# Strassen-type FFN products on one core: sums and forms on VectorE, raw weights in 512-column pieces, four pairs begun early

## The chip, the cores and the metric

The kernel runs on one NeuronCore of a Trainium2 chip. The metric is the device time of one execution in microseconds (us), smaller being better. The core has TensorE (PE, matrix products; PEld is its weight load), VectorE (DVE), ScalarE (ACT), GpSimd (POOL) and SyncE (SP, which here issues nearly all DMAs). Each engine works through its own instructions in order, and waits where an operand is not there yet.

## The reference

One layer of an encoder, for 512 prompt tokens and 256 sample tokens with the same weights, model width 1024, FFN width 2816, all in float32:

```python
x = layer_norm(ALPHA * x + 0.5 * swiglu(x, ffn1_up, ffn1_down), ln1_g, ln1_b)
u = x @ w_in
...
h_a = rwkv7_branch(u_a, ...) @ w_branch_a
h_b = retention_branch(u_b, pos) @ w_branch_b
mix = (sigmoid(gate_a) * h_a + sigmoid(gate_b) * h_b) @ w_out
x = layer_norm(ALPHA * x + mix, ln2_g, ln2_b)
x = layer_norm(ALPHA * x + 0.5 * swiglu(x, ffn2_up, ffn2_down), ln3_g, ln3_b)
```

with swiglu(x) = (silu(x W_gate) * (x W_up)) W_down. The prompt and the sample attend only within themselves.

## The kernel before

All tiles hold features on the 128 partitions and the T = 768 tokens (512 + 256, SEGS) along the columns; x is eight tiles z[0..7]. A float32 matrix product is made of three products of rounded parts: every operand is split into a high part (a cast on ACT, L187) and a low part (source minus high part on VectorE, L188), and PE multiplies high by high, high by low and low by high (mm3, mmt, L198). High and low parts are named xh/xl (tokens), ph/pl (weights), eh/el (forms of the tokens), hh/hl (hidden units) and wh/wl (weights of other stages).

The stages, by the trace's time: FFN1 (`first`, 0 to 525 us); LN1 with two leading input projections (to 581); the RWKV and retention preparation and the scan (to about 1240); `merge` with w_out and LN2 (to about 1432); FFN2 (to 1944); LN3 and the stores (to 1984). A scheduler orders each engine's instructions from the program's text and its own costs, so the order is not that of the text.

**FFN up products.** The gate and up weights of a block of hidden units and the tokens are cut into halves and multiplied by a Winograd form of Strassen's scheme: seven products in place of eight. For each of the 22 pairs j, `head(j)` makes product 11 and copies it to u; `second(j)` adds product 21 in the same PSUM bank and applies silu; `do_up(j)` makes four sums of raw weights (`combine`, tiles sa, on POOL, L329), then products T1, T3, T2, 22 and T4, five adds of 384 columns on VectorE (L360), a product of 768 columns (L371) and the split into hh and hl. Each product is 12 matmuls of 384 columns. `forms` (L276 to L291) makes for each of the four k four forms of the tokens, two on POOL (L282, L283) and two on VectorE (L284, L285), and splits them.

**FFN down products.** Chunks of 6, 6, 5 and 5 pairs: after the first pair of the next chunk, `do_down` adds the chunk's share of all eight z. The last chunk's down product is made per token segment (`last_down`), with LN's token sums behind it. Weights split for the first segment are held for the second (KEEP = 4 in a pool of their own, and two more in the rotating pool).

**Buffers.** Raw up weights have three buffers wr of 1024 columns (512 KB, one DMA each); the four sums have buffers sa; ph and pl four each. The pools fw (raw, sums, split weights) and xe (forms) are closed before the last down, whose weights come through another pool, wp. Before the loop over chunks, two pairs have head and second done in FFN1, four in FFN2 (LEAD2). In PSUM, mm tiles are two banks wide (down products), pc one bank (up products and token sums); FFN1 and the preparation, and `merge` and FFN2, have different shares of the eight banks.

**LN.** Mean and variance are sums over all features, so over the partitions of eight tiles: either eight adds on VectorE into acc (L246) and one product with a matrix of ones on PE (L248), or eight such products on PE (L239). MPE and VPE say which, by LN and token segment. Then 1/sqrt on ACT and VectorE (L230 to L234), the scaling (L267 on VectorE, L268 on ACT) and, for LN1, stores of x to DRAM (x1d) and the split of x.

## Time and profile before

| | us |
|---|---|
| median of 3 runs (lowest, highest) | 1990.48 (1988.84, 1992.99) |
| the profiled execution | 1985.87 |
| its span, first to last instruction | 1984.1 |
| PE busy in the span | 1870.1 (94%) |
| DVE busy | 1240.4 (63%) |
| ACT busy | 833.2 (42%) |
| POOL busy | 486.5 (25%) |

The mean granted TensorE clock is 0.971 of full speed. A busy share is an average over stages with different limits, so the table alone does not say what a change is worth: that is read from the windows (busy time and counts in stretches of the span), from the chain of waits (the work that ended last, followed back) and from single rows of the timeline. In a row, the part in square brackets is the idle time of that engine just before and what ended it.

### The profile page before, as it was taken

The numbers are of one execution on the slowest core, as the hardware profiler recorded it, in microseconds if no ns is written. First come the engines' busy times: TensorE is split into PE (matmuls) and PEld (weight loads), VectorE is DVE, ScalarE is ACT, GpSimd is POOL, SyncE is SP. The second block draws the span as 40 slices with busy tenths as digits, with TensorE's granted clock in tenths as the row PEclk, the third lists the DMA queues.
The fourth block names the chain that finished last, engine by engine and source line by source line (L and its number), as shares of the span: only waits on it lengthen the run. The fifth ranks groups of instructions, "written<-read, shape, count | busy, mean of one in ns | idle before, by whom it ended". The sixth has DMA issues, their size and how long they took to land.

```text
span 1984.1 us, 33432 instructions
## 1 busy us (share of the span) xinstructions
PE 1870.1 (94%) x13224; PEld 1681.4 (85%) x13224; DVE 1240.4 (63%) x2064; ACT 833.2 (42%) x1512; POOL 486.5 (25%) x482
## 2 busy tenths in 40 slices
PE   6999999999979999999999988999779999999996
PEld 6999999999758777887888777789679999899985
DVE  8753745646675786768445556487777456365567
ACT  4432423424364453445355645334644234243334
POOL 5412303222000264445510000000164033131310
PEclk8999999999989999999999989999889999999998
DMA  4221221221242433333464442554222212212122
GB/s 133 75 67 62 76 74 64 61 78 46 79 143 86 148 117 127 109 129 116 142 207 127 128 114 90 196 194 146 75 76 72 78 64 71 69 64 74 65 68 73
DMA packets 115100, 197.48 MB, mean 100 GB/s; under 512 B 52736, under 2 KB 61312, under 8 KB 114944
## 3 DMA queue, kind: packets, MB, share of 16 engines
q1 hardware_dynamic: 97408, 173.32, 27.5%
q0 software_dynamic: 3424, 14.94, 2.3%
q10 hardware_dynamic: 14112, 7.08, 1.3%
q8 instruction: 105, 1.72, 0.4%
q14 instruction: 51, 0.42, 0.1%
HBM read 153.62 MB, written 41.68 MB: 98 GB/s over the span
## 4 chain that ended last, share of the span: by engine, by line
PE 81%; DVE 8%; ACT 4%; DMA 3%; issue 2%; POOL 1%; ACTq 0%; SPq 0%; DVEq 0%; POOLq 0%
PE mm L198 39%; PE pc L198 30%; PE pc L102 2%; PE mm L464 2%; ACT z L268 1%; PE pc L891 1%; POOL sa L329 1%; PE w L827 1%; PE w L838 1%; PE pc L939 1%; DMA wr<-in_f2u 1%; DVE z L259 1%; PE w L832 1%; PE pc L521 1%; DMA t<-gd 1%
## 5 line engine op out<-in xcount | busy, mean ns | idle before, releaser
L198 PE MATMUL pc<-xh,ph 128*128 128x384 f32 x704 | 241.4, 343 | 30.4 <-ACT xh L187 12.9
L187 ACT CAST ph<-wr 128x512 fp32r<-128x512 f32 (+1 forms) x228 | 129.1, 568 | 300.5 <-PE mm L198 180.2
L188 DVE TENSOR_TENSOR pl<-wr,ph 128x512 fp32r<-128x512 f32 (+1 forms) x228 | 174.7, 768 | 125.3 <-ACT ph L187 109.6
L198 PE MATMUL pc<-xl,ph 128*128 128x384 f32 x704 | 240.1, 341 | 0.2 <-DVE xl L188 0.2
L329 POOL TENSOR_TENSOR sa<-wr 128x512 f32<-128x512 f32 x44 | 70.1, 1593 | 626.5 <-DMA wr<-in_f1u 290.2
L360 DVE TENSOR_TENSOR u<-u,pc 128x384 f32<-128x384 f32 x220 | 121.0, 550 | 161.5 <-PE pc L198 160.0
L198 PE MATMUL mm<-xh,wh 128*128 128x512 f32 (+1 forms) x672 | 188.2, 356 | 18.1 <-ACT xh L187 8.5
L187 ACT CAST ph<-sa 128x512 fp32r<-128x512 f32 x176 | 109.2, 621 | 222.5 <-PE pc L198 160.0
L198 PE MATMUL mm<-xl,wh 128*128 128x512 f32 (+1 forms) x672 | 180.5, 346 | 2.6 <-DVE xl L188 2.6
L198 PE MATMUL pc<-eh,ph 128*128 128x384 f32 x528 | 178.0, 338 | 4.4 <-DVE u L360 4.1
L198 PE MATMUL pc<-el,ph 128*128 128x384 f32 x528 | 177.5, 336 | 0.2 <-DVE el L188 0.2
L188 DVE TENSOR_TENSOR pl<-sa,ph 128x512 fp32r<-128x512 f32 x176 | 143.3, 816 | 48.6 <-ACT ph L187 28.0
L198 PEld LDWEIGHTS pc<-xh,ph 128*128 128x128 f32 x704 | 135.9, 193 | 33.7 <-ACT xh L187 13.6
L158 ACT CAST wh<-wr 128x1024 fp32r<-128x1024 f32 (+2 forms) x96 | 85.7, 892 | 179.7 <-PE mm L198 133.0
L159 DVE TENSOR_TENSOR wl<-wr,wh 128x1024 fp32r<-128x1024 f32 (+2 forms) x96 | 100.9, 1051 | 93.4 <-PE mm L198 41.3
L198 PE MATMUL pc<-xh,pl 128*128 128x384 f32 x704 | 152.3, 338 | 3.1 <-DVE pl L188 3.1
L198 PEld LDWEIGHTS mm<-xh,wh 128*128 128x128 f32 x672 | 107.4, 192 | 42.6 <-ACT xh L187 9.7
L198 PE MATMUL mm<-hh,ph 128*128 128x512 f32 (+1 forms) x544 | 138.9, 336 | 0.0
L198 PE MATMUL mm<-hl,ph 128*128 128x512 f32 (+1 forms) x544 | 138.8, 336 | 0.0
L198 PEld LDWEIGHTS pc<-xl,ph 128*128 128x128 f32 x704 | 135.9, 193 | 0.6 <-DVE xl L188 0.6
L198 PE MATMUL mm<-xh,wl 128*128 128x512 f32 (+1 forms) x672 | 134.1, 348 | 0.0
L198 PEld LDWEIGHTS pc<-xh,pl 128*128 128x128 f32 x704 | 126.2, 190 | 3.7 <-DVE pl L188 3.7
(290 smaller groups left out, 4108.3 us busy)
## 6 DMA issues: line engine op xcount, KB each, us to landing
wr<-in_f2u SPq DMA_DIRECT2D x48, 512.0 KB, 3.5
wr<-in_f1u SPq DMA_DIRECT2D x44, 512.0 KB, 3.4
wr<-in_w_in SPq DMA_DIRECT2D x32, 512.0 KB, 3.5
wr<-in_w_out SPq DMA_DIRECT2D x16, 512.0 KB, 3.6
wr<-in_w_in SPq DMA_DIRECT2D x28, 256.0 KB, 3.4
wr<-in_f1d SPq DMA_DIRECT2D x16, 384.0 KB, 3.2
dd<-ar SPq DMA_DIRECT2D x8, 768.0 KB, 3.3
dd<-kb SPq DMA_DIRECT2D x8, 768.0 KB, 3.9
```

The lines of the kernel that those rows point to most:

```text
L102: self.nc.tensor.matmul(ps, w, x[:, a:b], start=True, stop=True)
L158: nc.scalar.copy(hi, raw)
L159: nc.vector.tensor_tensor(out=lo, in0=raw, in1=hi.bitcast(F32), op=ALU.subtract)
L187: self.nc.scalar.copy(hi, src)
L188: self.nc.vector.tensor_tensor(out=lo, in0=src, in1=hi.bitcast(F32), op=ALU.subtract)
L198: self.latest = self.nc.tensor.matmul(o, w, x[:, a:b], start=start and i == 0, stop=stop and i == len(terms) - 1, skip_group_check=more).ins
L259: nc.vector.tensor_tensor(out=z[k][:, a:b], in0=z[k][:, a:b], in1=mean, op=ALU.subtract)
L268: nc.scalar.activation(zk, zk, AF.Identity, bias=self.vcol(g0 + 8 + k), scale=self.vcol(g0 + k))
L329: nc.gpsimd.tensor_tensor(out=t, in0=a, in1=b, op=op)
L360: add = lambda o, a, b: nc.vector.tensor_tensor(out=o, in0=a, in1=b, op=ALU.add)
L464: nc.tensor.matmul(dst, x[:, ts], w[:, :, k % 4], start=(k == 0 and q == 0), stop=(k == KT - 1 and q == 2))
L521: nc.tensor.matmul(op, v[:, a // P + j], x[:, j, :n], start=(j == 0 and q == 0), stop=(j == nj - 1 and q == 2))
```

## The change

- `combine` and all of `forms` run on VectorE (L355 and L290 after the change). `forms` goes form by form over the four k, and each form is split in a piece of its own of 384 columns.
- Raw weights come in pieces of 512 columns (256 KB) in ten buffers (RAWS): `raw` issues two DMAs where it issued one of 1024 columns (L329). First halves of the early pairs are loaded again when the pair goes on.
- Four pairs are begun early in both FFNs (LEAD). The constants' preparation (`then`) is put behind the first chunk.
- The up products use mm tiles too: `pairps` gives one two-bank tile for products 11 and T2 and one for T1 and T3; for the early pairs T2 has a pc bank. PSUM shares stay the same from FFN1 into the preparation (mm 2, pc 2, and one tile in pre) and from `merge` into FFN2 (mm 3, pc 2).
- fw and xe stay open to the end of the block. The last down's weights go through the raw buffers and hp tiles (8 of each, 5 of which hold hidden units): three split weights are held for the second segment, not six. The two leading projections after LN1 take their split weights from the xe tiles, and are written in `first`; wp is made after FFN1.
- LN scratch comes from the tiles sa and wr. Token sums: the mean of the 256-token segment in LN1 and LN3, and the variances of both segments in LN1 and of the 512-token segment in LN3, move from VectorE to eight products with ones on PE (35 more products).
- KEEPO: one w_out tile is kept between the three token blocks of `merge`, not two.

```diff
-MPE = {1: (0, 0), 2: (0, 0, 0), 3: (0, 0)}
-VPE = {1: (0, 0), 2: (0, 0, 1), 3: (0, 1)}
+MPE = {1: (0, 1), 2: (0, 0, 0), 3: (0, 1)}
+VPE = {1: (1, 1), 2: (0, 0, 1), 3: (1, 1)}
...
-LEAD2 = 4
-KEEPO = 2
+LEAD = 4
+RAWS = 10
+KEEPO = 1
...
+    def pairps(self):
+        self.turn += 1
+        p = self.pre if self.pre and self.turn % (self.pb["mm"] + 1) == 0 else self.ps
+        t = p.tile([P, 2, 512], F32, tag="mm", name=self.nm("mm"), bufs=1 if p is self.pre else self.pb["mm"])
+        return t[:, 0, :TH], t[:, 1, :TH]
...
+        m = KT // 2
+        sub = lambda o, a, b: nc.vector.tensor_tensor(out=o, in0=a, in1=b, op=ALU.subtract)
+        B = [[t[:, c:c + TH] for t in (z[k], z[k + m]) for c in (0, TH)] for k in range(m)]
+        ta = [tmp.tile([P, T], F32, tag="hh", name=self.nm("f")) for k in range(m)]
+        for k, (b11, b12, b21, b22) in enumerate(B):
+            sub(ta[k][:, :TH], b12, b11)
+            self.split(ta[k][:, :TH], *(t[:, TH:] for t in xs[k]))
+        tb = [tmp.tile([P, T], F32, tag="hl", name=self.nm("f")) for k in range(m)]
+        for k, (b11, b12, b21, b22) in enumerate(B):
+            sub(tb[k][:, :TH], b22, b12)
+            self.split(tb[k][:, :TH], *(t[:, :TH] for t in ext[k]))
+        for k, (b11, b12, b21, b22) in enumerate(B):
+            sub(ta[k][:, TH:], b22, ta[k][:, :TH])
+            self.split(ta[k][:, TH:], *(t[:, 2 * TH:] for t in ext[k]))
+        for k, (b11, b12, b21, b22) in enumerate(B):
+            sub(tb[k][:, TH:], b21, ta[k][:, TH:])
+            self.split(tb[k][:, TH:], *(t[:, TH:2 * TH] for t in ext[k]))
...
-        hp = self.pool(ctx, "hp", max(CHUNKS) + 3, "right")
-        hs, kept, raws, open_ = {}, {}, {}, {}
+        hp = self.pool(ctx, "hp", max(CHUNKS) + 2, "right")
...
-        cu = ctx.enter_context(ExitStack())
-        fw, xe = self.pool(cu, "fw", 1), self.pool(cu, "xe", 1)
+        xe, fw = self.pool(ctx, "xe", 1), self.pool(ctx, "fw", 1)
+        lp = fw, ("sa", "wr"), (4, RAWS)
...
         def raw(src):
-            t = fw.tile([P, D], F32, tag="wr", name=self.nm("wr"), bufs=3)
-            n = src.shape[1] * src.shape[2]
-            nc.sync.dma_start(t[:, :n].rearrange("p (a b) -> p a b", b=P), src)
-            return t[:, :n]
+            out = []
+            for a in range(0, src.shape[1], m):
+                part = src[:, a:min(a + m, src.shape[1])]
+                t = fw.tile([P, m * P], F32, tag="wr", name=self.nm("wr"), bufs=RAWS)[:, :part.shape[1] * P]
+                nc.sync.dma_start(t.rearrange("p (a b) -> p a b", b=P), part)
+                out.append(t)
+            return out
+        def wide(src, h, l):
+            for i, t in enumerate(raw(src)):
+                c = slice(i * m * P, i * m * P + t.shape[-1])
+                self.split(t, h[:, c], l[:, c])
+            return tuple(t.rearrange("p (a b) -> p a b", b=P) for t in (h, l))
...
-            nc.gpsimd.tensor_tensor(out=t, in0=a, in1=b, op=op)
+            nc.vector.tensor_tensor(out=t, in0=a, in1=b, op=op)
...
-            ps = self.bank()[:, :TH]
-            product(ps, g[:, :m * P], "11", True)
+            ps, pb = self.pairps()
+            product(ps, g[0], "11", True)
...
-            pc, pd, pb = (self.bank()[:, :TH] for _ in range(3))
+            pc, pd = self.pairps()
+            if early:
+                pb = self.bank()[:, :TH]
...
+        def last_weights(n):
+            w = len(chunks[-1]) * P
+            return wide(down[n, :, chunks[-1][0]:chunks[-1][-1] + 1],
+                        *(hp.tile([P, T], F32R, tag=t, name=self.nm("w"))[:, :w] for t in ("hh", "hl")))
...
-            fetch = lambda n, keep=None: self.wtile(down[n, :, ch[0]:ch[-1] + 1], (len(ch), P), keep)
-            for i, (n, w) in enumerate(self.reuse(kept, fetch, kp, KEEP)):
+            order = [n for n in held] + [n for n in range(KT) if n not in held]
+            now = dict(held)
+            for i, n in enumerate(order):
+                w = now[n] if n in held else last_weights(n)
+                now[n] = w
...
-            return mean
+            return mean, {n: now[n] for n in order[KT - (max(CHUNKS) + 2 - len(ch)):]}
...
-            if lead > 2:
-                raws.pop((j, 0))
-        if then:
-            then()
+            raws.pop((j, 0))
...
-        cu.close()
-        self.weights(wctx, D)
-        lp, kp = self.pool(ctx, "lp", 4), self.pool(ctx, "kp", KEEP)
+            if then and ci == 0:
+                then()
+        held = {}
         for seg in BLK[idx]:
-            after(seg, last_down(seg, lp, kp), lp)
+            mean, held = last_down(seg, held)
+            after(seg, mean, lp)
+
+        def lead_weights(i, src):
+            return wide(src, *(xe.tile([P, D], F32R, tag=f"{t}{i}", name=self.nm("w")) for t in ("eh", "el")))
+
+        return lead_weights
...
+            kp = self.pool(ctx, "kp", KEEPO)
             tq = self.pool(ctx, "tq", TQ)
             mp = self.pool(ctx, "mp", 8, "right")
-            kp = self.pool(ctx, "kp", KEEPO, "right")
...
-                self.psum(cw, pre, mm=1, pc=4)
+                self.psum(cw, pre, mm=2, pc=2)
...
-                    self.first(ctx, cm)
-            with ExitStack() as cw:
-                self.psum(cw, pre, mm=2, pc=2)
+                    self.first(ctx)
+                self.weights(cm, D)
...
+            self.psum(cx, mm=3, pc=2)
...
-            self.psum(cx, mm=2, pc=4)
...
-        self.ffn(ctx, z, xs, 1, I["f1u"], I["f1d"], after, 2, inputs, wctx, self.consts)
+        weights = self.ffn(ctx, z, xs, 1, I["f1u"], I["f1d"], after, LEAD, inputs, self.consts)
+        lead = self.lead = [self.mmps() for _ in range(2)]
+        lw = [weights(i, I["w_in"][12 + i]) for i in range(2)]
+        var = self.summed
+        with self.tc.issue_after(self.mean):
+            self.mm3(lead[0], lw[0], self.xs, SEGS[:1])
+        self.tc.add_manual_dep(var, self.latest.name, mybir.DependencyInfo(
+            mybir.DependencyClass.NoSync, mybir.DependencyReason.DATA), reason="order")
+        with self.tc.issue_after(var):
+            self.mm3(lead[1], lw[1], self.xs, SEGS[:1])
+        for ps, w in zip(lead, lw):
+            self.mm3(ps, w, self.xs, SEGS[1:])
```

In rows of instructions, PE goes from 10006 to 10041, DVE from 1983 to 2146, ACT from 1476 to 1520, POOL from 487 to 295, SP from 482 to 666.

Three places of the engines' orders follow. The first is the start of FFN1: before the change POOL, in the last forms and the first sums (f: forms, z: token tiles, wr: raw weights, sa: sums).

```order
L283 TENSOR_TENSOR f_161<-z_79,z_75 128x384
L283 TENSOR_TENSOR f_173<-z_80,z_76 128x384
L283 TENSOR_TENSOR f_185<-z_81,z_77 128x384
L283 TENSOR_TENSOR f_197<-z_82,z_78 128x384
L329 TENSOR_TENSOR sa_315<-wr_313 128x512
L329 TENSOR_TENSOR sa_317<-wr_116,wr_313 128x512
```

After it, VectorE, where the forms end and the first sums stand (el: low half of a form, pl: low half of a weight, vm: a constant).

```order
L290 TENSOR_TENSOR f_183<-z_82,f_167 128x384
L195 TENSOR_TENSOR el_115<-f_167,eh_114 128x384
L195 TENSOR_TENSOR el_109<-f_180,eh_108 128x384
L195 TENSOR_TENSOR pl_343<-wr_335,ph_342 128x512
L355 TENSOR_TENSOR sa_384<-wr_380,wr_382 128x512
L195 TENSOR_TENSOR el_111<-f_181,eh_110 128x384
L195 TENSOR_TENSOR pl_360<-wr_337,ph_359 128x512
L355 TENSOR_TENSOR sa_386<-wr_376,wr_380 128x512
L139 TENSOR_TENSOR vm<-vec_1102 128x14
```

Forms, sums and splits now stand in one queue, and the sums of the first pair behind nearly all forms.

The second is SP around LN1. Before the change (wr of in_w_in: projection weights; the first two rows are the leading projections', the third that of the projection after them):

```order
L157 DMA wr_5072<-in_w_in 128x1024
L157 DMA wr_5078<-in_w_in 128x1024
L157 DMA wr_5232<-in_w_in 128x1024
L452 DMA wr_5293<-in_w_in 128x512 x2
L274 DMA x1d<-z_75 128x512
L274 DMA x1d<-z_76 128x512
```

After the change, from the end of the 16 stores of x1d (the leading projections' loads, four of 512 columns, stand ahead of the stores):

```order
L285 DMA x1d<-z_82 128x256
L119 DMA cos_5344<-in_cos 128x512
L119 DMA sin_5346<-in_sin 128x512
L535 DMA G_5887<-in_ret 128x896
L119 DMA g_5357<-in_g 128x512
L610 DMA lora_5411<-in_lora 128x2x128
L164 DMA wr_5415<-in_w_in 128x1024
```

The weight of the projection that follows the leading ones (wr_5232, now wr_5415) has moved from ahead of the stores to behind them.

The third is VectorE in LN3, with L259 (after: L270) the centring, L267 (L278) the scaling, L400 (L435) the add of a down product to z. Before:

```order
L400 TENSOR_TENSOR z_12770<-z_12770,mm_19213 128x256
L246 TENSOR_TENSOR acc_19109<-acc_19109,z_12770 128x256
L259 TENSOR_TENSOR z_12769<-z_12769,pc_19074 128x256
L259 TENSOR_TENSOR z_12770<-z_12770,pc_19074 128x256
...
L234 SCALAR_TENSOR_TENSOR ln_19042<-ln_19043,ln_19042 128x512
L267 SCALAR_TENSOR_TENSOR z_12769<-z_12769,ln_19042 128x512
```

After:

```order
L435 TENSOR_TENSOR z_12955<-z_12955,mm_19546 128x256
L241 SCALAR_TENSOR_TENSOR sa_19365<-sa_19366,sa_19365 128x512
L278 SCALAR_TENSOR_TENSOR z_12952<-z_12952,sa_19365 128x512
...
L278 SCALAR_TENSOR_TENSOR z_12959<-z_12959,sa_19365 128x512
L435 TENSOR_TENSOR z_12956<-z_12956,mm_19574 128x256
L270 TENSOR_TENSOR z_12952<-z_12952,pc_19397 128x256
```

The centring of the 256-token segment has moved from ahead of the scaling of the 512-token segment to behind it, and so has the last add.

More of the change, by code (lines that the diff above doesn't have):

```diff
@@ L238, in token_sum @@
         if pe:
-            nc.tensor.matmul(st["ps"], self.ones, src, start=k == 0, stop=k == KT - 1)
+            self.summed = nc.tensor.matmul(st["ps"], self.ones, src, start=k == 0, stop=k == KT - 1).ins
             return
@@ L244, in token_sum @@
         if k == 1:
-            st["acc"] = pool.tile([P, TP], F32, tag="acc", name=self.nm("acc"), bufs=2)[:, :src.shape[-1]]
+            st["acc"] = self.scratch(pool, 1)[:, :src.shape[-1]]
         nc.vector.tensor_tensor(out=st["acc"], in0=st["src"] if k == 1 else st["acc"], in1=src, op=ALU.add)
@@ L277, in forms, with ffn @@
         nc = self.nc
-        for k in range(KT // 2):
-            (b11, b12), (b21, b22) = ([t[:, :TH], t[:, TH:]] for t in (z[k], z[k + KT // 2]))
-            ta, tb = (tmp.tile([P, T], F32, tag=t, name=self.nm("f")) for t in ("hh", "hl"))
-            t1, t2, t3, t4 = ta[:, :TH], ta[:, TH:], tb[:, :TH], tb[:, TH:]
-            nc.gpsimd.tensor_tensor(out=t1, in0=b12, in1=b11, op=ALU.subtract)
-            nc.gpsimd.tensor_tensor(out=t3, in0=b22, in1=b12, op=ALU.subtract)
-            nc.vector.tensor_tensor(out=t2, in0=b22, in1=t1, op=ALU.subtract)
-            nc.vector.tensor_tensor(out=t4, in0=b21, in1=t2, op=ALU.subtract)
-            self.split(t1, *(t[:, TH:] for t in xs[k]))
-            self.split(tb, *(t[:, :2 * TH] for t in ext[k]))
-            self.split(t2, *(t[:, 2 * TH:] for t in ext[k]))
-    def ffn(self, ctx, z, xs, idx, up, down, after, lead, first, wctx, then=None):
+        m = KT // 2
[15 more added lines that the diff above has]
+            self.split(tb[k][:, TH:], *(t[:, TH:2 * TH] for t in ext[k]))
+    def ffn(self, ctx, z, xs, idx, up, down, after, lead, first, then=None):
         nc = self.nc
@@ L379, in do_down @@
             for n in range(KT):
-                r = raw(down[n, :, ch[0]:ch[-1] + 1])
-                parts = [pieces(r[:, a:min(a + m * P, len(ch) * P)]) for a in range(0, len(ch) * P, m * P)]
+                parts = [pieces(t) for t in raw(down[n, :, ch[0]:ch[-1] + 1])]
                 ps = self.mmps()
```

40 lines of the change are left out of this document (16 added, 24 removed).

## Prediction

> **What bounds the kernel now.** I read the busy time by 50 us windows first (columns: window, then busy time and count of PE, PEld, DVE, ACT, POOL, then granted clock, DMA share, GB/s).
>
> ```profile
> 0.00:50.00 50.00, 32.30 (x132) 30.11 (x132) 40.63 (x61) 25.12 (x46) 26.23 (x21) 0.83 0.41 133
> 200.00:250.00 50.00, 50.00 (x291) 50.00 (x290) 36.11 (x49) 22.64 (x39) 21.77 (x15) 1.00 0.25 82
> 500.00:550.00 50.00, 42.82 (x232) 36.08 (x230) 37.21 (x66) 16.20 (x23) 0.00 (x0) 0.96 0.28 82
> 1400.00:1450.00 50.00, 35.47 (x191) 31.36 (x189) 40.55 (x85) 35.45 (x73) 11.78 (x9) 0.86 0.23 74
> 1450.00:1500.00 50.00, 41.43 (x218) 39.72 (x219) 37.49 (x45) 17.32 (x29) 33.88 (x20) 0.90 0.26 87
> ```
>
> In the middle of each FFN the PE is full at clock 1.00, about 290 matmuls in 50 us, 0.172 us each, and no helper engine can be worth anything there. The time lies at the edges: both FFN starts, LN1, and LN3 at the end. Next the chain of waits (start, length, what), at the two FFN starts:
>
> ```profile
> 38.51 4.37 POOL sa L329
> 127.00 3.14 PE mm L198 x18
> 1437.58 5.02 POOL f L283 x4
> 1442.60 5.66 issue
> 1448.25 9.78 POOL sa L329 x3
> 1460.16 4.66 DMA wr<-in_f2u
> 1546.63 3.14 PE mm L198 x18
> ```
>
> The first down product ends the first chunk: 564 up matmuls stand ahead of it in either FFN (6 pairs of 84, and 60 of the seventh), 97.2 us at 0.172. So the FFNs run as if they had begun, without a gap, at 127.00 - 97.2 = 29.8 and 1546.63 - 97.2 = 1449.4. Call this the effective start. The first up matmuls ran at 7.05 and 1428.63, so each start loses some 20 us.
>
> **The starts.** The rows of the timeline (start, length, engine, line, operation, tile, count, idle before and what ended it) say why:
>
> ```profile
> 20.97 0.69 PE L198 MATMUL pc<-xh,ph 128*128 128x384 f32 x1 [6.32 <-ACT u L337]
> 31.75 0.69 PE L198 MATMUL pc<-xh,ph 128*128 128x384 f32 x1 [3.67 <-ACT ph L187]
> 11.53 5.10 POOL L282 TENSOR_TENSOR f<-z 128x384 f32<-128x384 f32 x4 [11.07 <-DMA z<-in_xT]
> 11.58 2.92 DVE L188 TENSOR_TENSOR pl<-wr,ph 128x512 fp32r<-128x512 f32 x2 [0.44 <-ACT ph L187]
> 18.24 1.34 DVE L284 TENSOR_TENSOR f<-z,f 128x384 f32<-128x384 f32 x1
> 23.23 1.60 POOL L329 TENSOR_TENSOR sa<-wr,wr 128x512 f32<-128x512 f32 x1
> 28.30 0.55 DVE L284 TENSOR_TENSOR f<-z,f 128x384 f32<-128x384 f32 x1
> 35.10 0.68 DVE L188 TENSOR_TENSOR pl<-sa,ph 128x512 fp32r<-128x512 f32 x1
> 1428.63 0.66 PE L198 MATMUL pc<-xh,ph 128*128 128x384 f32 x1 [5.83 <-ACT xh L187]
> 1455.81 0.69 PE L198 MATMUL pc<-xh,ph 128*128 128x384 f32 x1 [5.82 <-ACT ph L187]
> ```
>
> A 128x384 form costs VectorE 1.34 us while POOL works and 0.55 (0.47 from start to start) when it rests; the same form costs POOL 1.28 (5.10 for four), a weight sum 1.60. After the change POOL is silent here, so I price VectorE at 0.47 for 384 columns and 0.60 for 512 (a 0.68 us row, less the same overlap of 0.08).
>
> FFN1: from 11.58, VectorE has up to the low half of the first T1 weight 36 operations of 384 and 9 of 512: 16.9 + 5.4 = 22.3 us, with the constants' small ones about 23, so T1 is fed at about 35. Meanwhile PE runs four early pairs (96 matmuls) rather than two; the first copy lets PE go on at about 17.8 and not 20.97, since no cast ahead of it on ACT waits for POOL. Of the four early products' PSUM tiles there are three: the fourth head waits for the first silu, which stands behind the eh casts on ACT, about 24; VectorE is at the third pair's low half by then (24.7), so this costs nothing more. 108 matmuls are done at about 35.6: 35.6 - 18.6 = 17.0. Then each early pair asks VectorE for 4 sums and 5 low halves (9 x 0.60), 5 adds of 384 (2.4) and two operations of 768 columns (about 0.88 each): 9.5 to 10.2 us against 60 x 0.172 = 10.3 of PE. That is tight; I add 2 for stalls. Effective start 19, **gain 11** (bounds 5 and 13: with the slow 1.34 form in half the places, and with no stall).
>
> FFN2: LN2's last scaling frees VectorE at about 1432.3. Up to the first T1 low half come 30 operations of 384, four of 256 (0.34), five of 512: 18.5 us, 1450.8; the four sums of the first pair are made earlier, under LN2. PE does three heads from 1428.63, waits for the copies until 1439, does three seconds, waits to 1446 for the first silu, and has 132 matmuls done at about 1456.7: 1456.7 - 22.8 = 1434, plus 2.5 of stalls, 1436.5 to 1437.5. **Gain 12** (bounds 5 and 15). The POOL chain (9.78) and the DMA waits of the sums disappear: ten 512-column buffers are free where three of 1024 columns were being turned over.
>
> **The middle.** Per pair VectorE gains 4 sums (2.4 us) and gets about 11.4 of the 14.5 PE needs (84 x 0.172); sums stand most of a pair ahead of their product in VectorE's order, and the add in front of each waits for a product that PE has finished several microseconds before the next use. In the window at 200 the 15 POOL operations would bring 15 x 0.68 = 10.2 to 36.11: 46.3 of 50. **Zero**, with PE's own work as cover; without it, a rival below. Early pairs' first halves are loaded twice (16 DMAs of 256 KB): also 0.
>
> By the Trainium skill, "DMA: Bandwidth & Descriptors", sections "Anatomy of one DMA" and "Rules for kernel authors", a transfer has a fixed part of about 2 us and should be large, at least 1 MiB; an estimate by its formula is 2.6 us for a 256 KB piece and 3.2 for 512 KB, so two pieces one after another would cost 5.2 where one transfer cost 3.2. This case's issue rows show no difference:
>
> ```profile
> wr<-in_f1u SPq DMA_DIRECT2D x44, 512.0 KB, 3.4
> wr<-in_w_in SPq DMA_DIRECT2D x28, 256.0 KB, 3.4
> ```
>
> Half the bytes land after the same 3.4 us, so I take it as latency that overlaps; were it serial, it is the rival further down.
>
> **FFN1's end and LN1.**
>
> ```profile
> 491.13 3.92 issue
> 494.23 0.72 ACT L158 CAST wh<-wr 128x640 fp32r<-128x640 f32 x1 [1.95 <-DMA wr<-in_f1d]
> 495.05 0.77 PE L198 MATMUL mm<-hh,wh 128*128 128x512 f32 x1 [3.92 <-issue]
> 496.04 0.63 PE L198 MATMUL mm<-hh,wh 128*128 128x512 f32 x1
> 498.97 0.39 PE L198 MATMUL mm<-hh,wh 128*128 128x512 f32 x1
> 553.21 0.79 PE L198 MATMUL mm<-xh,wh 128*128 128x512 f32 x1 [7.10 <-ACT xh L187]
> 527.53 16.37 SPq L157 DMA_DIRECT2D wr<-in_w_in  x3
> 576.09 1.05 SPq L274 DMA_DIRECT2D x1d<-z  x2
> 579.74 0.88 SPq L497 DMA_DIRECT2D G<-in_ret  x1
> 581.39 0.51 PE L198 MATMUL mm<-xh,wh 128*128 128x512 f32 x2
> ```
>
> The weight of the last down is already in a raw buffer, so PE restarts as soon as hh is cast: about 3.0 us after the up products rather than 3.92, 0.9 gained. The variance sums by ones-matmuls replace adds on VectorE; the lead's inputs come about 2.5 us sooner. But the third w_in load, for the projection at 581.39, was issued at about 544, ahead of the x1d stores. Now only the two lead tiles are. The third goes behind 16 x1d stores, cos, sin, G, g and a lora load on SP: issued at about 579.74 + 2 - 2.5 = 579.4, landed 3.5 later, cast 0.9: PE starts at about 584 where it started at 581.4, with the next w_in loads queued behind it. That is +2.4, and about 1.5 for a clock that has dropped in the gap (after 495.05 the matmuls took 0.63 instead of 0.39, at half the pace, for some 3 us). Sum **+3** (bounds -3, if the DMA queue drains earlier, and +6).
>
> By the Trainium skill, "TensorE: Matmul & The Clock Gate", section "Part 1: The HAM clock gate", the clock halves after an idle window of about 3.4 us. The trace agrees at 495.05, after 3.92 us; an estimate by the rule is that a 3.0 us gap may escape, 1.5 us better at each of two restarts, which I leave out of the sum.
>
> **Prep, scan, merge.** One w_out tile fewer is kept, so two more loads: **+1** (0 to 2; one load is 3.5 us with a buffer to spare). Their engines' work is unchanged.
>
> **The tail.**
>
> ```profile
> 1944.35 0.69 DVE L400 TENSOR_TENSOR z<-z,mm 128x512 f32<-128x512 f32 x1 [2.09 <-PE mm L198]
> 1962.83 1.83 PE L248 MATMUL pc<-acc,ones 128*128 128x512 f32 x4
> 1964.70 2.74 DVE L259 TENSOR_TENSOR z<-z,pc 128x256 f32<-128x256 f32 x8 [0.79 <-PE pc L248]
> 1965.63 4.75 PE L239 MATMUL pc<-ln,ones 128*128 128x256 f32 x16 [0.96 <-ACT ln L261]
> 1969.60 4.90 DVE L267 SCALAR_TENSOR_TENSOR z<-z,ln 128x512 f32<-128x512 f32 x8
> 1973.03 8.25 ACT L268 ACTIVATE z<-z,vec 128x512 f32<-128x512 f32 x14
> ```
>
> Count from T1 = 1944.2, the end of the 512-column products. Before, the last z is out at 1981.28, T1 + 37.1, and the 256-column centring (1964.70) and variance run beside the 512-column scaling. After, three tiles are held instead of six, so five are loaded and split again on ACT and VectorE, each cast ahead of a square. The ones-matmuls bring the 512 variance at about T1 + 19.6, as before (20.4), but VectorE's order now puts all eight 512-column scalings ahead of the last z add and the 256-column centring: scalings T1 + 23.6 to 28.4, mean 29.8, centring to 32.5, its variance (4.75) from 30.6 to 35.4, a table load 1.28, rsqrt 2, scalings 2.7, last z about T1 + 41.4. That is +4.3, less 0.9 at the restart: **+3.5** (bounds +1 and +6).
>
> **Sum:** -11 - 12 + 0 + 3 + 1 + 3.5 = -15.5. The profiled execution took 1985.87 (span 1984.1 and 1.77 around it): 1970.4. The runs' median is 1990.48, 4.6 above it, so I predict **1975**, -0.8%. Less than 0.2%, 4 us, I call no change.
>
> **Rivals.**
> 1. Early pairs stay helper-bound. For it: the tight 10.2 against 10.3. If VectorE needs 12 us a pair, 1.7 is lost eight times, 13.6 in all, and the gain is 2: 1988. Against: every slow row has POOL beside it. 14%, time 1980 to 1990.
> 2. More is gained: both starts at their upper bounds (13 + 15), LN1 and tail at their lower (-3, +1): 1990.5 - 29 = 1961; half way there 1967. For it: POOL's absence speeds every VectorE operation. 12%.
> 3. Slower: VectorE becomes the bound in the middle. The point is 36.11 + 15 d = 50, d = 0.93 us per sum. If a sum with two SBUF inputs costs 1.34, as the form beside POOL did, a 50 us window needs 56.2; 36 ordinary pairs of 14.5 us are 522 us, 12.4% of them 65: 1975 + 65 = 2040. Against: 0.68 for the low half, also with two SBUF inputs. 7%.
> 4. Slower: pieces land one after another. Four at 3.4 us are 13.6 per early pair against 10.3: 3.3 x 8 = 26, 2001. For it: the 4.66 us DMA wait in the chain. Against: with three buffers that wait is one for a buffer, and four pieces in 10.3 us are 102 GB/s, under the 133 of the first window. 5%.
>
> **Chances.** The forecast has 62%, its own range 1968 to 1983. Rival 1 lies half within 0.2%. Faster by over 0.2%: 0.62 + 0.12 + half of rival 1, 0.79 after a little for the unknown; same 0.09; slower 0.12. The range, 1963 to 1992, leaves out rivals 3 and 4 and the far end of 2.
>
> **What would show it.** First down product near 116 in FFN1 and about 14 us sooner, measured from the first up matmul, in FFN2; no POOL row in either FFN; low halves at 0.68 throughout; windows in the middle still at 290 matmuls. LN1's loss would show as a PE wait on wr or wh near 570 to 575, and the tail as a longer stretch from the last 512-column product to the end. It is wrong if the middle windows fall below 285, or if PE waits on sa or pl in pairs 1 to 4.

## The result and the profile after

| | before | after |
|---|---|---|
| median of the runs shown together, us | 1991.74 (4 runs, 1988.84 to 1993.7) | **2166.55** (4 runs, 2163.26 to 2167.14) |
| ratio, with its 95% interval | | **1.0876 [1.0857, 1.0894]** |
| span of the profiled execution, us | 1984.1 | 2161.5 |
| mean granted clock | 0.971 | 0.952 |

Forecast was 1975, in a range of 1963 to 1992; the change makes the kernel 8.8% slower. I cut both spans at five places that the two timelines share: the first matmul of the last down in FFN1, the first projection after the two leading ones, the first matmul on yh in `merge`, the first up matmul of FFN2, and the first matmul of its last down.

| stage, us | before | after | difference | predicted |
|---|---|---|---|---|
| FFN1 to its last down | 495.05 | 571.46 | +76.4 | -11 |
| last down, LN1, lead | 86.34 | 90.57 | +4.2 | +3 |
| preparation and scan | 686.14 | 687.28 | +1.1 | +1, with the next |
| merge and LN2 | 161.10 | 171.41 | +10.3 | |
| FFN2 to its last down | 486.01 | 566.44 | +80.4 | -12 |
| last down, LN3, end | 69.46 | 74.34 | +4.9 | +3.5 |
| sum | 1984.1 | 2161.5 | +177.4 | -15.5 |

So the loss is in the two FFNs, and twice nearly the same. The view by windows of the changed kernel (window, then busy time and count of PE, PEld, DVE, ACT, POOL, granted clock, DMA share, GB/s) tells where in them:

```profile
0.00:50.00 50.00, 38.54 (x191) 35.88 (x192) 44.56 (x95) 30.91 (x60) 0.21 (x4) 0.97 0.65 220
150.00:200.00 50.00, 49.99 (x288) 45.66 (x288) 23.90 (x37) 11.44 (x21) 0.00 (x0) 1.00 0.25 80
200.00:250.00 50.00, 39.63 (x208) 38.67 (x206) 28.81 (x46) 16.16 (x28) 0.00 (x0) 0.93 0.16 51
250.00:300.00 50.00, 41.17 (x202) 40.03 (x203) 24.03 (x38) 15.28 (x26) 0.00 (x0) 0.87 0.13 37
```

The first window is as hoped: 191 matmuls where there were 132, and no POOL. A window of mostly down products (150) is full too. The windows that the prediction had named as its test, those of ordinary pairs, hold 208 and 202 matmuls (the two shown) and not 290, at a clock of 0.93 and 0.87 in the place of 1.00. VectorE is no bound there: it is busy for 28.81 of 50 us, with all the sums, where it was busy for 36.11 before (fewer pairs run through such a window now). Nor is DMA, at 0.16.

The waits of PE in the changed kernel (engine and line, what released it, us in total, times, longest) name what ends its idle time, and the group of the first matmuls on forms (busy, mean ns | idle before it and what ended it) says which matmul stands still:

```profile
PE mm L205 <- ACT u L363: 123.1, 33, 4.4
```

```profile
L205 PE MATMUL mm<-eh,ph 128*128 128x384 f32 x496 | 181.5, 366 | 115.6 <-ACT u L363 114.3 <-DVE u L388 1.3
```

L363 is `head`'s copy of product 11 to u. Before, PE was not held by that copy in the middle at all. One pair of the changed kernel, row by row (start, length, engine, line, operation, tile, count, idle before and what ended it), reads as follows; L388 is the add of a product, L399 the product of 768 columns, L194 and L195 the split. PE's earlier matmuls and weight loads, a DMA issue, an earlier cast and two later VectorE rows (a sum and the low half of hh) are left out:

```profile
205.74 1.03 PE L205 MATMUL mm<-eh,pl 128*128 128x384 f32 x5
206.63 0.56 DVE L388 TENSOR_TENSOR u<-u,mm 128x384 f32<-128x384 f32 x1 [3.22 <-PE mm L205]
207.11 0.68 DVE L195 TENSOR_TENSOR pl<-sa,ph 128x512 fp32r<-128x512 f32 x1
207.71 0.69 DVE L195 TENSOR_TENSOR pl<-wr,ph 128x512 fp32r<-128x512 f32 x1
208.31 0.95 DVE L399 TENSOR_TENSOR u<-u,u 128x768 f32<-128x768 f32 x1
209.35 0.83 ACT L194 CAST hh<-u 128x768 fp32r<-128x768 f32 x1 [2.79 <-DVE u L399]
210.09 0.47 ACT L363 COPY u<-mm 128x384 f32<-128x384 f32 x1
210.61 0.45 PE L205 MATMUL mm<-eh,ph 128*128 128x384 f32 x1 [3.84 <-ACT u L363]
...
230.88 0.45 PE L205 MATMUL mm<-eh,ph 128*128 128x384 f32 x1 [3.84 <-ACT u L363]
```

PE ends T4 of pair j at 206.7. VectorE then adds it (L388), makes two low halves that stand ahead in its queue, and multiplies (L399). ACT, idle for 2.79 us, may only now cast hh of pair j; the copy of product 11 of pair j+1 stands *behind* that cast in ACT's queue, though PE made that product four products earlier (22, T1, T3 and T4 lie between in PE's order). PE's next matmul is the first of T2 of pair j+1, and it waits for the copy. The same 3.84 us come back 20.27 us later, where a pair needs 14.5 without a gap. The chain of waits shows the same loop pair after pair (start, length, what):

```profile
81.63 0.55 DVE u L388
82.19 0.60 DVE pl L195
82.79 0.88 DVE u L399
...
84.48 0.48 ACT u L363
...
85.01 16.25 PE mm L205 x83
```

Why does T2 wait for a copy of product 11? In the changed kernel `pairps` gives both the two halves of one two-bank tile. A half is a bank of its own, and T2 writes nothing that the copy reads; the wait comes with the shared tile, as the experiments below show. The period is 5.8 us longer: 3.84 of gap, and about 1.9 for matmuls behind it, which run at 0.32 us from start to start for a few microseconds rather than 0.172, with a granted clock that falls as above. By the Trainium skill, "TensorE: Matmul & The Clock Gate", section "Part 1: The HAM clock gate", the clock halves after an idle window of about 3.4 us; the trace agrees with that, at gaps of 3.84 us.

Before, the copy stood behind the hh cast too, as ACT's timeline there shows:

```profile
215.33 0.84 ACT L187 CAST hh<-u 128x768 fp32r<-128x768 f32 x1 [0.89 <-DVE u L371]
216.07 0.62 ACT L187 CAST ph<-wr 128x512 fp32r<-128x512 f32 x1
216.59 0.47 ACT L337 COPY u<-pc 128x384 f32<-128x384 f32 x1
```

There the copy ended at 217.06, but T2 had a bank of its own, and PE ran through at a period of 14.56 (hh at 200.77, 215.33, 229.89). So the order on ACT is not new. What is new is that PE waits for it.

### The profile page after: what moved, and what is told of

Its sections match the earlier page's. It is cut to its first block, busy times and chain, and to the rows that moved or that the text cites. A ratio compares the mean times of both kernels' runs of the same rounds, so it can differ in the third digit from the quotient of the medians.

```text
span 2161.5 us, 33773 instructions
## 1 busy us (share of the span) xinstructions
PE 1941.8 (90%) x13294; PEld 1736.3 (80%) x13294; DVE 1279.1 (59%) x2265; ACT 845.4 (39%) x1556; POOL 191.8 (9%) x290
## 4 chain that ended last, share of the span: by engine, by line
PE 79%; DVE 10%; ACT 4%; issue 3%; DMA 3%; SPq 0%; ACTq 0%; DVEq 0%; POOLq 0%
PE mm L205 67%; PE mm L502 2%; PE pc L109 2%; DVE pl L195 1%; PE pc L250 1%; DVE u L399 1%; PE pc L918 1%; PE w L854 1%; PE pc L205 1%; ACT z L279 1%; ACT u L363 1%; PE w L865 1%; DMA wr<-in_w_in 1%; PE pc L559 1%; DMA t<-gd 1%
## 5 line engine op out<-in xcount | busy, mean ns | idle before, releaser
L205 PE MATMUL mm<-eh,ph 128*128 128x384 f32 x496 | 181.5, 366 | 115.6 <-ACT u L363 114.3
L194 ACT CAST ph<-wr 128x512 fp32r<-128x512 f32 (+1 forms) x228 | 129.6, 568 | 365.4 <-PE mm L205 348.1
L205 PE MATMUL mm<-xh,ph 128*128 128x384 f32 x704 | 247.3, 352 | 20.1 <-ACT u L363 8.8
L388 DVE TENSOR_TENSOR u<-u,mm 128x384 f32<-128x384 f32 x212 | 117.1, 553 | 249.6 <-PE mm L205 246.2
L205 PE MATMUL mm<-xl,ph 128*128 128x384 f32 x704 | 243.7, 346 | 0.3 <-DVE xl L195 0.3
L194 ACT CAST ph<-sa 128x512 fp32r<-128x512 f32 x176 | 109.5, 622 | 260.6 <-PE mm L205 239.7
L195 DVE TENSOR_TENSOR pl<-wr,ph 128x512 fp32r<-128x512 f32 (+1 forms) x228 | 141.7, 623 | 110.7 <-ACT ph L194 61.2
L205 PEld LDWEIGHTS mm<-eh,ph 128*128 128x128 f32 x496 | 100.0, 202 | 125.8 <-ACT u L363 123.9
L205 PE MATMUL mm<-el,ph 128*128 128x384 f32 x496 | 179.8, 362 | 0.0
L205 PEld LDWEIGHTS mm<-xh,ph 128*128 128x128 f32 x704 | 140.4, 200 | 27.1 <-ACT u L363 9.8
L195 DVE TENSOR_TENSOR pl<-sa,ph 128x512 fp32r<-128x512 f32 x176 | 121.2, 690 | 67.3 <-PE mm L205 66.8
L205 PE MATMUL mm<-xh,pl 128*128 128x384 f32 x704 | 146.9, 337 | 1.8 <-DVE pl L195 1.7
L205 PEld LDWEIGHTS mm<-xl,ph 128*128 128x128 f32 x704 | 139.6, 198 | 1.2 <-DVE xl L195 1.0
L205 PEld LDWEIGHTS mm<-xh,pl 128*128 128x128 f32 x704 | 125.3, 190 | 2.5 <-DVE pl L195 2.5
```

Source lines behind the costliest of these rows:

```text
L194: self.nc.scalar.copy(hi, src)
L195: self.nc.vector.tensor_tensor(out=lo, in0=src, in1=hi.bitcast(F32), op=ALU.subtract)
L205: self.latest = self.nc.tensor.matmul(o, w, x[:, a:b], start=start and i == 0, stop=stop and i == len(terms) - 1, skip_group_check=more).ins
L388: add = lambda o, a, b: nc.vector.tensor_tensor(out=o, in0=a, in1=b, op=ALU.add)
```

## The experiments

Two theories stood after the result. **A, the shared tile:** T2 waits for the copy of product 11 since both are one PSUM tile. **B, VectorE:** with the sums and forms in its queue, VectorE comes too late with the low halves and the multiplication, and the copy is only where that shows. Both predict the rows above. All ratios are to the kernel before, run again beside each group of experiments on the same chip.

### T2 in a bank of its own

The first kernel is the change with T2 always in a pc bank, as it had it for early pairs; T1 and T3 still share a tile.

```diff
-            if early:
-                pb = self.bank()[:, :TH]
+            pb = self.bank()[:, :TH]
```

> The changed kernel, with product T2 of every pair in a pc bank of its own (as the early pairs have it), not in the second half of product 11's tile. Theory A (T2 must wait until ACT has copied product 11 out of the shared tile, and that copy stands on ACT behind the previous pair's hh cast): the 3.84 us waits of PE for ACT u in the ordinary pairs are gone, the middle windows return to about 290 matmuls in 50 us, and the time falls by some 190 to about 1975, which is the prediction's sum. Rival B (VectorE, now with the sums, brings the pair's products late, and the copy is only where it shows): PE waits as long as before, for pl or u, and the time stays above 2100.

It took 2042.25 us, 1.0263 [1.0239, 1.0286]: 124 of the 175 us are gone by one line that gives VectorE nothing less to do. The window and the largest waits of PE in it:

```profile
200.00:250.00 50.00, 44.22 (x243) 41.42 (x241) 31.68 (x51) 18.41 (x32) 0.00 (x0) 1.00 0.18 53
```

```profile
PE mm L205 <- ACT u L363: 23.4, 19, 3.8
...
PE mm L205 <- DVE u L387: 11.6, 16, 0.7
...
PE mm L205 <- ACT u L370: 8.8, 15, 0.7
```

The long gaps are replaced by several of 0.6 to 0.9 us a pair, and the clock is 1.00 again: these short gaps do not cost the clock. Theory A holds for the larger part, but 243 matmuls are not 290, and the time is 67 us above the 1975 that it gave.

### The hh cast on POOL

Here the shared tile stays, and what stands ahead of the copy on ACT is taken away: the high half of hh is made on POOL.

```diff
-            self.split(s, *hs[j])
+            nc.gpsimd.tensor_copy(hs[j][0], s)
+            nc.vector.tensor_tensor(out=hs[j][1], in0=s, in1=hs[j][0].bitcast(F32), op=ALU.subtract)
```

> The changed kernel, tile still shared, but the hh cast of each pair runs on POOL and not on ACT, so that the copy of product 11 no longer stands behind it on ACT. Theory A: the wait shrinks from 3.84 to under 1 us, 1980 to 2010 (POOL's casts slow some VectorE operations to 1.3 us). Rival C (a bank whose neighbour in the same tile is being read is slow by itself, wherever the copy stands): the wait stays near 3.8 and the time near 2166. Rival B: unchanged or slower, since VectorE's low half of the hidden units then waits for a slower cast.

2040.4 us, 1.0247 [1.0219, 1.0275]. Moving one cast out of ACT's queue brings as much as T2's own bank: the wait for the copy falls from 123.1 to 16.0 us, though the copy still reads the neighbouring half. Some 2 us a pair remain (a period of 16.7 and not 14.56 us), so it stays 30 us above the range expected. The loop therefore needs both links, the tile that joins T2 to the copy and the cast that the copy stands behind.

```profile
PE mm L205 <- DVE u L388: 26.0, 24, 2.4
PE mm L205 <- ACT u L363: 16.0, 33, 4.9
```

### The sharing alone, in the kernel before

Nothing else of the change is made: sums and forms stay on POOL and VectorE as they were, raw weights come in three buffers. `pairps` is added, used for 11 with T2 and T1 with T3, with the change's PSUM shares.

```diff
...
-            ps = self.bank()[:, :TH]
+            ps, pb = self.pairps()
...
-            pc, pd, pb = (self.bank()[:, :TH] for _ in range(3))
+            pc, pd = self.pairps()
+            if early:
+                pb = self.bank()[:, :TH]
...
-                self.psum(cw, pre, mm=1, pc=4)
+                self.psum(cw, pre, mm=2, pc=2)
...
-            self.psum(cx, mm=2, pc=4)
+            self.psum(cx, mm=3, pc=2)
```

> The kernel before with one part of the change alone: products 11 and T2, and T1 and T3, share two-bank mm tiles (mm 2 and pc 2 in FFN1, mm 3 and pc 2 in FFN2). Sums and forms stay on POOL, raw weights in three pieces of 1024 columns. Theory A: 36 ordinary pairs wait some 4 us or more each, with a slowed clock behind it, 2140 to 2200. Rival B: no VectorE load is added, so 1985 to 2000.

2248.76 us, 1.1296 [1.1268, 1.1324]. The sharing alone costs 258 us, more than the whole change and more than expected, and with VectorE relieved of all it was to carry; of the 264 us by which the profiles differ, 253 lie in the two FFNs.

```profile
PE mm L204 <- ACT u L343: 188.0, 34, 7.1
```

```profile
200.00:250.00 50.00, 43.04 (x233) 40.90 (x232) 23.07 (x30) 14.09 (x24) 16.77 (x12) 0.90 0.16 53
```

It is the same wait (L343 is the copy here), 5.5 us a time where the change has 3.7. Its rows tell why it is longer:

```profile
234.65 1.67 DVE L194 TENSOR_TENSOR pl<-sa,ph 128x512 fp32r<-128x512 f32 x1
236.24 1.74 DVE L194 TENSOR_TENSOR pl<-wr,ph 128x512 fp32r<-128x512 f32 x1
237.91 2.01 DVE L379 TENSOR_TENSOR u<-u,u 128x768 f32<-128x768 f32 x1
241.27 0.69 PE L204 MATMUL mm<-eh,ph 128*128 128x384 f32 x1 [6.95 <-ACT u L343]
334.24 0.45 PE L204 MATMUL mm<-eh,ph 128*128 128x384 f32 x1 [3.83 <-ACT u L343]
```

From 234.5 to 241 POOL makes four sums, and the three VectorE operations ahead of the hh cast take 5.4 us together where the change's three rows had 2.3. Ahead of 334.24 POOL is silent, the same three take 0.68, 0.68 and 0.95 us, and the wait is that of the change. So VectorE's speed does set the length of the loop, and here it is POOL that slows it; but theory B, under which this kernel should be near 1990, is refuted as the cause.

### The sums back on POOL, twice

The other half of B: if VectorE were late, giving the four sums back to POOL should help. It was tried beside T2's own bank, and later beside banks of their own for all products (the kernel of the next section).

```diff
-            nc.vector.tensor_tensor(out=t, in0=a, in1=b, op=op)
+            nc.gpsimd.tensor_tensor(out=t, in0=a, in1=b, op=op)
```

> The first of these kernels (T2 in a bank of its own) with the weight sums back on POOL; forms stay on VectorE. Theory A: the middle is full in both, so only the two starts differ: POOL makes four sums at about 1.5 us a pair beside VectorE, 5 to 15 us slower than the first kernel, 1980 to 1990. Rival B: faster than the first kernel by 50 us or more, since VectorE is relieved.

> The kernel with all up products in banks of their own, and the weight sums back on POOL. Theory A: 5 to 15 us slower than with the sums on VectorE, from the two starts alone. Rival B: faster than it by 20 us or more.

Beside T2's own bank: 2037.91, 1.0234 [1.0209, 1.0258], against 1.0263 [1.0239, 1.0286] without it: the intervals overlap, so at best a little. Neither is the gain of 50 us that B asked for. Beside banks for all: 2013.06, 1.0116 [1.009, 1.0142], against 1.0074 [1.0056, 1.0092]: 9 us slower in the medians, though the intervals just touch. The profiles put it at the starts: FFN1 takes 5.0 us more and FFN2 5.2, and the first down product is at 123.2 and not 118.16. Where PSUM is out of the way, the sums are better on VectorE.

### Banks of their own for all up products

The change with the PSUM of before: every product of `head` and `do_up` in a pc tile of one bank. The pools must be laid out anew for that, and the preparation gets a share that neither kernel has.

```diff
...
-            ps, pb = self.pairps()
+            ps = self.bank()[:, :TH]
...
-            pc, pd = self.pairps()
-            if early:
-                pb = self.bank()[:, :TH]
+            pc, pd, pb = (self.bank()[:, :TH] for _ in range(3))
...
+                    self.psum(ctx, pre, pre2, pc=4)
...
-                self.psum(cw, pre, mm=2, pc=2)
+                self.psum(cw, pre, pre2, mm=1, pc=2)
...
+            self.psum(cx, mm=2, pc=4)
```

> The changed kernel with the PSUM shapes of the kernel before (every up product in a one-bank pc tile: pc 4 in FFN1 and FFN2); sums, forms, raw pieces, early pairs, held pools and LN sums as in the change. Theory A (each two-bank tile that two products share is held and released as one, so a product waits for the other half's reader): the waits of the first kernel of this study for u (0.58, 0.74 and 0.87 us a pair) are gone too, middle windows at 290 matmuls, 1970 to 1982. Rival B (VectorE with the sums is too late): it stays at 2020 to 2045.

2004.12 us, 1.0074 [1.0056, 1.0092]: the middle is full again, and the stage table becomes -9.1 (FFN1), +4.9, +12.3, +15.9, -11.8 (FFN2), +6.4. The time is above the 1970 to 1982 expected, for what the preparation and `merge` lose.

```profile
200.00:250.00 50.00, 50.00 (x291) 50.00 (x290) 35.95 (x60) 22.16 (x37) 0.00 (x0) 1.00 0.19 54
```

```profile
118.16 3.14 PE mm L201 x18
```

VectorE does 60 operations there where it did 49 and is busy for 35.95 us instead of 36.11. Both FFN starts show the gain that was forecast: the first down product runs at 118.16, where it ran at 127.00. Against the change, FFN1 is 85.5 us shorter and FFN2 92.3: that, 177.8 together, is the price of the shared tiles (and of the number of tiles that rotate, which goes with them). The +12.3 in the preparation is not the change's (which has +1.1 there) but comes with this kernel's own PSUM share; what exactly in that share costs it was not taken apart.

### T1 and T3 in one tile

To price the second shared tile alone, the last kernel with only T1 and T3 in the halves of one two-bank tile (`mmps2`, which is `mmps` with two halves of 512 columns):

```diff
...
-            pc, pd, pb = (self.bank()[:, :TH] for _ in range(3))
+            t, pb = self.mmps2(), self.bank()[:, :TH]
+            pc, pd = t[:, 0, :TH], t[:, 1, :TH]
```

> The kernel with all up products in banks of their own, except that T1 and T3 share one two-bank tile, as in the change. Theory A: waits of about 0.6 to 0.9 us for u return in each ordinary pair, 2000 to 2030. If the tile of T1 and T3 is harmless and only the three-tile turn of products 11 cost the rest, within 5 us of the kernel with all products in their own banks.

2032.36 us, 1.0214 [1.019, 1.0238]: 28 us more than with banks of their own. In the middle no gap is long, and the clock stays at 1.00:

```profile
200.00:250.00 50.00, 49.92 (x277) 47.47 (x276) 35.70 (x58) 21.11 (x36) 0.00 (x0) 1.00 0.18 53
```

```profile
PE mm L209 <- DVE u L391: 7.1, 10, 0.7
```

277 matmuls and not 291 in the same 50 us, and a pair every 15.4 us and not 14.56. The adds appear as a wait only ten times (0.7 us each); in the ordinary pairs the loss shows as late starts of a few tenths of a microsecond. That these are waits for the other half's reader is likely, but not shown row by row. So T2's tile costs the larger part (124 by the first experiment), T1's 28 by this one. They need not add up, since the kernels differ in how many tiles rotate.

### The LN sums as before

The change moved token sums of LN1 and LN3 from VectorE to PE. This kernel is the one with all banks of their own, with before's choice:

```diff
-MPE = {1: (0, 1), 2: (0, 0, 0), 3: (0, 1)}
-VPE = {1: (1, 1), 2: (0, 0, 1), 3: (1, 1)}
+MPE = {1: (0, 0), 2: (0, 0, 0), 3: (0, 0)}
+VPE = {1: (0, 0), 2: (0, 0, 1), 3: (0, 1)}
```

> The kernel with all up products in banks of their own, and LN's token sums as in the kernel before (means and variances of LN1, and of the 512-token segment of LN3, by adds on VectorE). The prediction's terms put LN1 at +3 and the tail at +3.5, of which the order that the ones-matmuls bring is a part: 2 to 6 us faster at the tail. If the order comes from the reloaded weights alone: no difference beyond 2 us, or slower by the adds.

2006.23 us, 1.0082 [1.0062, 1.0102]: no difference in all (1.0074). By one profile of each, the stage with LN1 takes 98.69 us and not 91.28, the tail 71.6 and not 75.9, but the preparation and `merge`, which this edit does not touch, are 7.6 us shorter too. So in the new buffers LN1 seems better off with its sums on PE and LN3 with them on VectorE, but the medians do not show it.

### `merge`: where the pool of kept weights stands

In the changed kernel PE waits in `merge` for yh, the split of t, and SP issues the second pair of loads of t only at 1350.35:

```profile
1362.56 1.65 PE L205 MATMUL mm<-yh,wh 128*128 128x512 f32 x3 [10.18 <-ACT yh L194]
1350.35 1.26 SPq L1011 DMA_DIRECT2D t<-ybd  x2
```

Before, there was no such wait, and the second pair was issued while the scan ran:

```profile
1231.77 1.95 SPq L984 DMA_DIRECT2D t<-ybd  x2
```

On SP it stood ahead of the four loads of w_b there, and stands behind them in the changed kernel. Beside KEEPO, the change moves the pool of kept w_out tiles in the text of `merge`, ahead of another pool and to the other side of SBUF; that line stands at the end of the diff, and the prediction gave it no price. This kernel is the one with all banks of their own (whose `merge` has the wait too, 11.7 us), with both as before, and lets the first projection take the tile that is free:

```diff
...
-KEEPO = 1
+KEEPO = 2
...
-            kp = self.pool(ctx, "kp", KEEPO)
...
+            kp = self.pool(ctx, "kp", KEEPO, "right")
...
+                self.turn = 1
```

> All up products in banks of their own, as two runs above, with two places mended: merge keeps two w_out tiles in a pool on the right as in the kernel before, and the preparation's first projection after the leading ones takes the free mm tile. Theory D (the pool of the w_out tiles moved ahead of merge's input tiles, these came to lie where the scan still worked, so the second half of ybd is loaded only after the scan): the 11.65 us wait of PE for yh goes, merge is 10 to 16 us shorter, and the preparation loses its 12 us; 1975 to 1985. Rival E (the yh wait comes from PSUM or from the order of loads on SP): merge stays some 15 us longer than before, 1990 to 2000.

1983.97 us, 0.9963 [0.995, 0.9976]. `merge` and LN2 take 163.8 us, not 176.99, and in this kernel's timeline the loads come while the scan still runs:

```profile
1227.19 1.03 SPq L1005 DMA_DIRECT2D t<-ybd  x2
1234.87 1.95 SPq L1005 DMA_DIRECT2D t<-ybd  x2
1272.09 0.49 PE L201 MATMUL mm<-yh,wh 128*128 128x512 f32 x1 [0.96 <-ACT gt L742]
```

Number of tiles and place of the pool were put back together; that the place decides was not tried by itself. It is inferred from the early loads, since the first load of w_out comes at 1322.80 in this kernel, long after these loads of t, and so cannot hold them up. The preparation was expected to lose its 12 us too, from the free tile; it still takes 9.1 us more than before. The next kernel adds before's LN3 sums to this:

```diff
-MPE = {1: (0, 1), 2: (0, 0, 0), 3: (0, 1)}
-VPE = {1: (1, 1), 2: (0, 0, 1), 3: (1, 1)}
+MPE = {1: (0, 1), 2: (0, 0, 0), 3: (0, 0)}
+VPE = {1: (1, 1), 2: (0, 0, 1), 3: (0, 1)}
```

> The kernel just named, with LN3's token sums as in the kernel before and LN1's as in the change. From the run with all LN sums as before, the stretch from the restart of PE to the end was 71.6 against 75.9 us, and LN1's was 7.4 longer: 3 to 5 us faster than the kernel just named.

1983.21 us, 0.9959 [0.9945, 0.9973]. The tail is 71.95 us in the profile where it was 75.3, but in the medians the two kernels cannot be told apart.

### The starts alone

Now the other way round: the kernel before, with only what the prediction had counted as gain. That is forms and sums on VectorE, form by form; raw weights in 512-column pieces, in eight buffers, not ten; four early pairs in FFN1. PSUM, pools, LN sums and `merge` are those of before.

```diff
+RAWS = 8
...
-            t = fw.tile([P, D], F32, tag="wr", name=self.nm("wr"), bufs=3)
...
+            for a in range(0, src.shape[1], m):
...
-            nc.gpsimd.tensor_tensor(out=t, in0=a, in1=b, op=op)
+            nc.vector.tensor_tensor(out=t, in0=a, in1=b, op=op)
...
-        self.ffn(ctx, z, xs, 1, I["f1u"], I["f1d"], after, 2, inputs, wctx, self.consts)
+        self.ffn(ctx, z, xs, 1, I["f1u"], I["f1d"], after, 4, inputs, wctx, self.consts)
```

> The kernel before with the parts alone that the prediction counted as gains: sums and forms on VectorE, raw pieces of 512 columns (eight buffers, since ten do not fit beside the other pools), four pairs begun early in FFN1. PSUM, pools, LN sums, loads of the last down and merge as before. The prediction's terms give -11 and -12: 1965 to 1972, ratio 0.987 to 0.991. Rival F (eight buffers are too few for four early pairs, or VectorE comes too late without the shared changes): 1980 to 1990.

**1966.32 us, 0.9872 [0.9859, 0.9885]**: 1.3% faster than the kernel before. By its stages, FFN1's last down begins 7.7 us sooner and FFN2 takes 12.25 us less, which is the span's 19.9; the other stages (+2.1, -3.8, +1.6 and +0.1) cancel. (The profiled execution of before, 1985.87, lies 6.3 us under the median of the runs beside this kernel, 1992.17, so the medians differ by 25.9.)

```profile
0.00:50.00 50.00, 36.96 (x183) 34.36 (x184) 42.93 (x92) 30.56 (x59) 0.22 (x4) 0.97 0.62 210
200.00:250.00 50.00, 50.00 (x290) 50.00 (x289) 35.48 (x58) 22.21 (x38) 0.00 (x0) 1.00 0.18 56
```

```profile
17.22 0.69 PE L199 MATMUL pc<-xh,ph 128*128 128x384 f32 x1 [3.78 <-ACT u L347]
1894.61 0.80 PE L199 MATMUL mm<-hh,wh 128*128 128x512 f32 x1 [3.89 <-ACT wh L159]
```

The last run has two early pairs in FFN1 rather than four, and is otherwise the same:

```diff
-        self.ffn(ctx, z, xs, 1, I["f1u"], I["f1d"], after, 4, inputs, wctx, self.consts)
+        self.ffn(ctx, z, xs, 1, I["f1u"], I["f1d"], after, 2, inputs, wctx, self.consts)
```

> The kernel just named with two early pairs in FFN1, as before, and four in FFN2. By the walk of the start, PE has 48 early matmuls less (8.3 us) to fill the time until VectorE has made the forms: 5 to 8 us slower than with four. If the forms come early enough for two pairs, within 2 us.

1971.43 us, 0.9902 [0.9887, 0.9916]: 5 us in the medians need the four pairs. By the profiles that is half of FFN1's gain (the first down product is at 123.24, against 119.33 with four and 127.00 before); the rest comes without them.

## Why the prediction was wrong

- **The middle, "Zero": the step that failed, by 178 us.** The cover that was named was VectorE's order alone: sums a pair ahead of their product, adds soon enough. That part was right, as the full windows with all sums on VectorE show. But the change also altered what PE waits *for*. `pairps` gave T2 the tile of product 11, and thereby a wait on ACT's copy; behind the copy stands the hh cast, behind that VectorE's product, behind that T4, which ends just before T2. The prediction used these tiles only to count the early heads' PSUM, and never asked who frees or reads either half, nor where the copy stands on ACT. Its own test, middle windows below 285, is what showed it wrong.
- **FFN1's start, -11: right in kind, nearly in size.** -8.8 at the first down product without the shared tiles (118.16 against 127.00; 116 was forecast), -7.7 with the starts alone. In the changed kernel itself the gain lies under the stalls. What is missing, 2 us, lies in the early pairs: they follow each other at 11.4 us, not 10.3, each with a wait for an add on VectorE, as in the kernel with banks of their own:

```profile
48.42 0.41 PE L201 MATMUL pc<-eh,ph 128*128 128x384 f32 x1 [0.74 <-DVE u L382]
```

It is not Rival 1, a busy VectorE: in the next two pairs VectorE sits idle for 1.32 us before that add, until PE's product is done. The two early pairs of before had the same wait. FFN1 now has four, so some 4 us, where 2 had been allowed; FFN2 had four already.

- **FFN2's start, -12: right,** -11.8 and -12.25 in the same two kernels.
- **LN1, +3: right mechanism.** +4.2. The estimate that a gap of 3.0 us may escape the slower clock held: after 3.09 us at 571.46 the matmuls take 0.39 us each, where after 3.92 us before they took 0.63. But the load of the projection's weight now stands behind the stores on SP, is issued at 655.46, and PE waits for its cast:

```profile
655.46 0.60 SPq L164 DMA_DIRECT2D wr<-in_w_in  x1
660.93 1.04 ACT L165 CAST wh<-wr 128x1024 fp32r<-128x1024 f32 x1 [4.78 <-DMA wr<-in_w_in]
662.03 1.00 PE L205 MATMUL mm<-xh,wh 128*128 128x512 f32 x2 [7.60 <-ACT wh L165]
```

- **Prep, scan, merge, +1: mis-sized.** Two loads of w_out were counted; +11.4 came, +10.3 of it in `merge`, where PE waits 10.18 us behind the second pair of loads of t, which is issued too late. The move of the pool, the likely reason, was in the code and had no price.
- **The tail, +3.5: right.** +4.9; all eight scalings of 512 columns stand ahead of the centring of 256, as the order had shown:

```profile
2138.31 4.91 DVE L278 SCALAR_TENSOR_TENSOR z<-z,sa 128x512 f32<-128x512 f32 x8
2144.77 2.74 DVE L270 TENSOR_TENSOR z<-z,pc 128x256 f32<-128x256 f32 x8 [1.22 <-PE pc L250]
```

- **The rivals** missed the mechanism too. Rival 3, VectorE bound in the middle, came nearest in sign and place, but the low half costs *less* than before (0.690 us a time, with POOL silent, against 0.816, rows below and in the last section), and there is no window of the middle in which VectorE is full. Rival 4, pieces one after another, is refuted: a 256 KB piece lands in 2.9 us, sooner than the 3.4 of in_w_in's pieces of the same size before, and with banks of their own PE's only waits in the early pairs, which take four pieces each, are for that add. Rival 2, more gain in all, is not what came.

```profile
L195 DVE TENSOR_TENSOR pl<-sa,ph 128x512 fp32r<-128x512 f32 x176 | 121.2, 690 | 67.3 <-PE mm L205 66.8 <-issue 0.4
```

```profile
wr<-in_f1u SPq DMA_DIRECT2D x96, 256.0 KB, 2.9
```

The estimate by the Trainium skill, "DMA: Bandwidth & Descriptors", section "Anatomy of one DMA", was 2.6 us; its formula is given there for DMAs that GpSimd issues, and these are SP's. The 2.9 of the rows lies between that and the 3.4 I took. The advice in the section "Rules for kernel authors" to keep transfers large (at least 1 MiB) is for bandwidth, and no bound here: the starts alone, with 256 KB pieces, are the fastest kernel, though the pieces were not tried by themselves.

The sum put right: 1985.87 - 9.1 - 11.8 + 177.8 + 4.2 + 1.1 + 10.3 + 4.9 = 2163.3, which is the changed kernel's profiled execution (2163.26). The term 177.8 is the difference of two profiled kernels, so this closes the account and is no forecast.

## What to carry to other kernels

A PSUM tile of two banks makes two products one object for the waits: each writer then waits for the readers of both halves, and for all that stands ahead of those readers in their queues. So for each product that changes its tile, look for the last reader of the whole tile and read that reader's queue up to it, on every engine and not only on the one that was given more work. And an edit that has no price in the sum (a pool moved, another PSUM share) should be tried by itself: here the parts that were meant to gain bring 26 us alone, and one part that was passed over costs 258 alone.
